# Hymba-style layer: window heads mixed side by side in one tile per token half, and four pieces of work in another order

## The chip, the cores and the metric

The kernel runs on one core of one Trainium2 chip. A core has a matrix engine (TensorE, here PE, with its weight loads as PEld), a vector engine (VectorE, DVE), a scalar engine (ScalarE, ACT), a general engine (GpSimd, POOL) and a synchronisation engine (SyncE, SP) that mostly issues transfers. Each runs its own list of instructions in order and waits on semaphores for the others. The metric is the device time of one execution in microseconds (us); lower is better.

## The reference

One layer over 1024 tokens of width 1024, in fp32. A normed input feeds one projection whose columns go to two token mixers: a sliding-window attention with 8 query heads in two groups of four, each group with one key/value head, and a 2-D neighbourhood attention with 8 heads. Then come an output projection, a gated MLP with a convolution of width 3 and a last norm.

```python
hn = rmsnorm(h, norm_mix[l])
proj = jnp.einsum('bsd,de->bse', hn, w_in[l])
qa, ka, va, qb, kb, vb = jnp.split(proj, splits, axis=-1)
qa = partial_rope(qa.reshape(B, S, A_HEADS, HEAD_DIM), cos, sin)
ka = partial_rope(ka.reshape(B, S, A_KV_HEADS, HEAD_DIM), cos, sin)
o_a = window_gqa_sink(qa, ka, va, sink[l])          # |i-j| <= 128, blocks of 128 tokens
o_b = neighbourhood_attention(qb, kb, vb, rpb[l])   # 16 x 64 grid, bias rpb per head
mix = jnp.concatenate([rmsnorm(o_a, norm_a[l]), rmsnorm(o_b, norm_b[l])], axis=-1)
h = h + jnp.einsum('bse,ed->bsd', mix, w_out[l])
hn = rmsnorm(h, norm_ffn[l])
h = h + conv_gated_mlp(hn, w_gate[l], w_up[l], conv_w[l], conv_b[l], w_down[l])
```

## The kernel before, in words

Everything is held transposed: channels on the 128 partitions, the 1024 tokens in the columns, two token halves of 512 columns. A projection job takes 128 output channels; its fp32 weight is split into a high part (`whi`, ACT, L156) and a low part (`wlo`, L157, DVE or POOL), and three matrix products (L172, L173, L174) add high by high, high by low and low by high. A job's weight comes in two halves of four input tiles: `load` and later `load_rest`. Jobs 0, 1 and 2 run before the window attention; the later jobs fill PE between attention steps.

The first three tiles are turned (the partial rotation) by a fold: L285 copies the rotating rows into a small tile `f` by DMA, DVE does four operations (L287 to L289), and L291 copies the rows back (`t<-f`). For the third tile the small tile is called `turns`. The SP queue issues most of these transfers, in its order. Then the tiles are split into high and low stacks: `split_first_k` (L316 to L319), `split_first` (L309, L310) and `split_pair` (L297 to L302).

A unit of window attention is a group g and a block b of 128 tokens. PE makes scores (L434), DVE takes a masked minimum with a bias (L464, result `nm`), ACT takes the exponential (L468) with its sum, DVE inverts it (L469, `sm`). The probabilities then go one of several ways to a 16-bit transposed pair: over POOL (L472, then L478, L479), over DVE (L482, L483, L485), over POOL with a scratch tile `y` (L488, L489), each to a transposing DMA (L490, `turned`), or, path T, over PE (L496) with ACT and DVE taking the result out of PSUM (L499, L500). PE multiplies by the values (L523), and `leave` adds the two 64-partition halves of the bank `o`: ACT copies two heads across (L534) and DVE adds two heads one at a time (L538) into tiles `mix[2g]` and `mix[2g+1]`, each 128 x 1024, named `mixa` in the profile.

The neighbourhood attention of a head h works the same way (L598 is its product with the values) with a bias tile `xb`, built by POOL from a gathered table in two subtractions (L556, L557). `bias_tiles(0)` is built early, and step 4 of head h asks for the tile of head h+1; `bias_tiles(1)` is also there early. Then follow the squares of the mixed heads (L211 through `squares`), the norm's gains (L871), a split into 16-bit halves (L200, L201) and the output projection.

PE's order is written out by hand, step by step. The orders of DVE, ACT, POOL and SP come from a scheduler that follows the program's order and priorities: `tc.high_priority` moves an instruction ahead, and `behind("name")` keeps what is in it behind a marked instruction in the engines' lists.

Of the kernel before, what the change touches and what calls it, by code (L numbers as in the profile page):

```python
# [17 lines left out]
AF = mybir.ActivationFunctionType  # L18
ALU = mybir.AluOpType
# [44 lines left out]
def hybrid_layer(tc, xT, w_in, w_out, w_gate, w_up, w_down, small, sink, rpb, consts, rope, out):  # L64
    nc = tc.nc
    with ExitStack() as ctx:
# [86 lines left out]
        def halve_w(raw):  # L153

            hi, lo = (wpool.tile([128, 4, 128], F32R, name=n, tag=n) for n in ("whi", "wlo"))
            mark["weights"] = nc.scalar.activation(hi, raw, AF.Copy)  # L156
            mark["weights low"] = (nc.gpsimd if mark.get("attention") or mark.get("early") else nc.vector).tensor_tensor(lo, raw, f32(hi[:, :, :]), op=ALU.subtract)  # L157
            return [(hi[:, j, :], lo[:, j, :]) for j in range(4)]

        def load_w(src):  # L160
# [116 lines left out]
        def rotate(t, n, order=()):  # L277

            m = slice(0, n)
            f, u = folded[0]  # L280
            folded.append(folded.pop(0))
            rows = lambda s: t[4 * s:n:8].rearrange("a (c w) -> a c w", w=128)
            fold = lambda s: f[m, s]
            for s in range(2):
                (nc.scalar, nc.sync)[s].dma_start(fold(s), rows(s))  # L285
            for s in range(2):
                nc.vector.tensor_tensor(u[m, s], f[m, 1 - s], rs[m, s], op=ALU.mult)  # L287
            nc.vector.tensor_tensor(f[m], f[m], rc[m], op=ALU.mult)
            mark["turned"] = nc.vector.tensor_tensor(f[m], f[m], u[m], op=ALU.add)  # L289
            with behind(*order):  # L290
                back = [nc.sync.dma_start(rows(s), fold(s)) for s in range(2)]  # L291
            mark["back"] = back[1]

        def split_pair(t, early=False):

# [88 lines left out]
            return [v[:, i].rearrange("p c s w -> p c (s w)") for i in range(n // 64)], up  # L384

        qa, ka, va, qb, kb, vb = {}, {}, {}, {}, {}, {}
        mix = [None] * 8

        def turn(m, t):
            g, i = divmod(m, 3)  # L390
# [59 lines left out]
        class Rows:  # L450
# [5 lines left out]
            def softmax(self, path, j, ps, n, bias, nsink=None, skip=0):  # L456

                c = n // 128
                with tc.high_priority(offset=50):
# [9 lines left out]
                    nc.vector.reciprocal(sm, sm)  # L469
                    x = apart(p[:, 0:n])  # L470
                    if path in "PT":
                        nc.gpsimd.tensor_scalar(x, x, sm, P_TOP, op0=ALU.mult, op1=ALU.mult)  # L472
                    if path == "T":
                        return lambda: self.turn(j, p, c, skip)
                    hl = staged()
# [26 lines left out]
        def unit_window(g, b):  # L502
# [26 lines left out]
            def leave():  # L529
                ot = apool.tile([128, 2, 128], F32, name="ot", tag="ot", bufs=1, padded_shape=[128, 4, 128])  # L530
                o4 = st["o"][:, :].rearrange("p (j w) -> p j w", w=128)
                for e in range(2):
                    me, other = slice(64 * e, 64 * e + 64), slice(64 - 64 * e, 128 - 64 * e)
                    nc.scalar.activation(ot[me], o4[other, e::2, :], AF.Copy)  # L534
                    for i in range(2):
                        if mix[2 * g + i] is None:
                            mix[2 * g + i] = big("mixa", "mix")
                        nc.vector.tensor_tensor(mix[2 * g + i][me, b * 128:(b + 1) * 128], o4[me, e + 2 * i, :], ot[me, i, :], op=ALU.add)  # L538

            return [q_step(j) for j in range(4)], [v_step(i, k) for k in range(2) for i in range(len(cs))], [lambda j=j: turn[j]() for j in range(4) if PATH_A[j] == "T"]  # L540

        def bias_tiles(h):

            raw = apool.tile([128, RAW_LEN], F32, name="rr", tag="rr", bufs=1)
            src = bass.AP(tensor=rpb.tensor, offset=rpb.offset + h * RPB_LEN, ap=[[RPB_W, ROWS], [1, 8], [1, RAW_LEN]])
            nc.sync.dma_start(raw, src)
            x = apool.tile([128, 5, 128], F32, name="xb", tag="xb")
            a = raw[:, 0:1]
            view = lambda d0, step, n: bass.AP(
                tensor=a.tensor, offset=a.offset + RAW_LEN - 1 - 8 * (d0 + 1),  # L550
                ap=[list(a.ap[0]), [-8 * step, n], [-RPB_W, ROWS], [-1, 8]])
            mk = cst[:, K_MB:K_MB + 384].rearrange("p (v r c) -> p v r c", r=ROWS, c=8)
            far = mk[:, 1:2]
            far = bass.AP(tensor=far.tensor, offset=far.offset, ap=[list(far.ap[0]), [0, 2], [8, ROWS], [1, 8]])
            xv = x[:, :, :].rearrange("p v (r c) -> p v r c", c=8)
            nc.gpsimd.tensor_tensor(xv[:, 1:4], mk, view(-1, 1, 3), op=ALU.subtract)  # L556
            nc.gpsimd.tensor_tensor(xv[:, 0::4], far, view(-1, 2, 2), op=ALU.subtract)  # L557
            return x

        bias_of = {}  # L560
# [63 lines left out]
        class Project:  # L624
# [10 lines left out]
            def run(self):  # L635
# [7 lines left out]
                else:  # L643

                    ps = [bank("pj", "pj") for _ in range(2)]
                    for h, k in [(h, i - 3 * h) for i in range(KT + 3) for h in range(2) if 0 <= i - 3 * h < KT]:
                        block(ps[h], self.w[k], xg[k], h, k == 0, k == KT - 1)
                        yield
                        if h and k % 2:
                            mg[k // 2] = split16(mix[k // 2], "xg")  # L650
                        if k == KT - 1:
                            with tc.high_priority(offset=500):
                                evacuate(self.t, ps[h], h, self.grid)
# [139 lines left out]
        for h in range(2):  # L793
            evacuate(third.t, ps3[h], h, False)
        with tc.high_priority(offset=400):
            with behind("turned"):
                turn(third.m, third.t)
            with behind("value"):
                nc.scalar.activation(warm, eps, AF.Exp)
# [25 lines left out]
        def rest():  # L825
            for i, job in enumerate(jobs[1:]):
# [15 lines left out]
                        aux[i, n]()  # L842
                if i == 0:
                    with behind("stack", "copied"):
                        mark["early"] = True
                        jobs[2].load_rest()
                        mark["early"] = False
                    with behind("weights"):
                        make_stacks(third)
                if isinstance(job, Project):  # L850
# [4 lines left out]
                        yield False  # L855

        def square_a():
            norm["sq"] = squares(mix[0:4], 2, ups[0:4])

        def narrow_a(h):  # L860
            norm["v", h] = inverse_power(norm["sq"][:, tsl(h)], 512, "pt")
# [5 lines left out]
            nc.scalar.activation(norm["a"][:, tsl(h)], widen(norm["v", h], "pt"), AF.Copy)  # L867

        def normed_a(i, h):
            x = lambda: mix[i][:, tsl(h)]  # L870
            return lambda: nc.vector.scalar_tensor_tensor(  # L871
                x(), x(), gains[:, i:i + 1], norm["a"][:, tsl(h)], op0=ALU.mult, op1=ALU.mult)

# [1023 lines left out]
```

## Time and profile before

| | |
|---|---|
| median of 3 runs | 1031.53 us (1031.27 to 1031.98) |
| profiled execution | 1031.43 us, its span 1029.6 us |
| granted clock of PE | 0.998 |
| PE busy | 1009.7 us (98%) |
| DVE busy | 878.2 us (85%) |
| ACT busy | 676.7 us (66%) |
| POOL busy | 216.6 us (21%) |

The stages by time, in the span: to about 58 us the first projections and folds; to about 200 us the window attention; from 181 to 343 us the neighbourhood attention beside it and after it, with projections between the steps; to about 413 us the output projection and its norm; then the gate, up and down products to the end. Times in the rows are from the span's start. A row's idle time is what stood empty before the instruction on its engine, with the engine, tile and line that ended it.

### The profile page before, as it was taken

Reading aid. Unit: us, or ns where it says so; the run is one execution under the profiler, and the core shown is the slowest. Engines: PE = TensorE matmul, PEld = TensorE weight load, DVE = VectorE, ACT = ScalarE, POOL = GpSimd, SP = SyncE. Lnnn points to the kernel's source line nnn. Section 1 sums busy time; section 2 is a strip of 40 time slices with the busy share of each in tenths; the row PEclk is TensorE's granted clock in tenths of the full one; section 3 lists DMA queues with packets and bytes.
Section 4 is the critical chain, followed back from the end, with each engine's and each line's share of the span. In section 5 each row is a group of like instructions: output and inputs, shape, how many; then the busy total and the mean of one; then the engine's idle time right before and its main releaser. Section 6 shows DMA issues by size and latency. Waiting matters only on the chain.

```text
span 1029.6 us, 15701 instructions
## 1 busy us (share of the span) xinstructions
PE 1009.7 (98%) x5102; PEld 576.6 (56%) x5102; DVE 878.2 (85%) x1746; ACT 676.7 (66%) x1242; POOL 216.6 (21%) x340
## 2 busy tenths in 40 slices
PE   8999999999999999999999999999999999999996
PEld 6877777777875545544444444444444444444446
DVE  7799998766898799899897988898888879999874
ACT  8567787768687587645777777754634657655551
POOL 2244555767876310001000000000000000000002
PEclk9999999999999999999999999999999999999999
DMA  8557474787699765201787867733232779978834
GB/s 319 191 136 138 100 152 99 146 167 133 138 192 219 261 251 194 83 1 42 235 276 250 273 233 256 235 113 133 82 113 102 256 243 307 308 244 268 258 140 164
DMA packets 143939, 191.80 MB, mean 186 GB/s; under 512 B 77360, under 2 KB 88112, under 8 KB 143856
## 3 DMA queue, kind: packets, MB, share of 16 engines
q1 hardware_dynamic: 133264, 164.84, 56.1%
q10 hardware_dynamic: 10592, 25.95, 6.5%
q8 instruction: 40, 0.66, 0.2%
q14 instruction: 43, 0.35, 0.1%
HBM read 132.81 MB, written 28.57 MB: 157 GB/s over the span
## 4 chain that ended last, share of the span: by engine, by line
PE 73%; DVE 5%; DMA 1%; ACT 1%; issue 1%; POOL 0%; ACTq 0%; DVEq 0%; POOLq 0%
PE dn L1185 6%; PE dn L1186 6%; PE dn L1187 6%; PE pj L180 6%; PE z L1185 5%; PE z L1186 5%; PE z L1187 5%; PE y L1185 4%; PE y L1186 4%; PE y L1187 4%; PE x L1185 4%; PE x L1186 4%; PE x L1187 4%; PE pj L172 2%; PE pj L174 2%; PE pj L173 2%
## 5 line engine op out<-in xcount | busy, mean ns | idle before, releaser
L1187 PEld LDWEIGHTS <-wlo 128*128 128x128 f16 x898 | 87.8, 98 | 101.4 <-issue 0.2
L1185 PEld LDWEIGHTS <-whi 128*128 128x128 f16 x898 | 88.1, 98 | 100.3
L1186 PEld LDWEIGHTS <-whi 128*128 128x128 f16 x898 | 87.8, 98 | 100.2
L1187 PE MATMUL dn<-xd,wlo 128*128 128x512 f16 (+1 forms) x330 | 120.4, 365 | 0.0
L1186 PE MATMUL dn<-xd,whi 128*128 128x512 f16 (+1 forms) x330 | 120.4, 365 | 0.0
L1185 PE MATMUL dn<-xd,whi 128*128 128x512 f16 (+1 forms) x330 | 120.4, 365 | 0.0
L172 PE MATMUL pj<-xgh,whi 128*128 128x512 f32 x248 | 106.7, 430 | 0.0
L1185 PE MATMUL z<-hg,whi 128*128 128x512 f16 x264 | 100.1, 379 | 0.0
L1186 PE MATMUL z<-hg,whi 128*128 128x512 f16 x264 | 100.1, 379 | 0.0
L1187 PE MATMUL z<-hg,wlo 128*128 128x512 f16 x264 | 100.1, 379 | 0.0
L468 ACT ACTIVATE p<-p,nm 128x385 f32<-128x385 f32 (+3 forms) x128 | 74.8, 585 | 36.8 <-DVE nm L464 33.9
L174 PE MATMUL pj<-xgh,wlo 128*128 128x512 f32 x248 | 97.9, 395 | 0.0
L173 PE MATMUL pj<-xgl,whi 128*128 128x512 f32 x248 | 97.4, 393 | 0.0
L1159 ACT ACTIVATE whi<-ws,m 128x512 f16<-128x512 f32 (+1 forms) x96 | 65.9, 708 | 37.9 <-DVE ws L1326 21.9
L1160 DVE SCALAR_TENSOR_TENSOR wlo<-ws,m,whi 128x512 f16<-128x512 f32 (+1 forms) x96 | 70.1, 739 | 20.4 <-ACT whi L1159 20.2
L1040 POOL TENSOR_TENSOR back<-back,cst 128x4 f32<-128x4 f32 (+1 forms) x7 | 2.8, 394 | 356.9 <-DVE back L1039 356.9
L1174 ACT ACTIVATE scan<-scan 128x1024 f32<-128x1024 f32 (+1 forms) x60 | 61.0, 1017 | 19.4 <-DMA scan<-in_w_down_dram 13.0
L1159 ACT ACTIVATE whi<-raw,m 128x512 f16<-128x512 f32 (+1 forms) x78 | 51.3, 699 | 18.1 <-DMA raw<-in_w_down_dram 11.2
L1160 DVE SCALAR_TENSOR_TENSOR wlo<-raw,m,whi 128x512 f16<-128x512 f32 (+1 forms) x78 | 55.3, 731 | 6.9 <-ACT whi L1159 6.8
L1187 PE MATMUL y<-hg,wlo 128*128 128x512 f16 x160 | 60.6, 379 | 0.0
L1185 PE MATMUL y<-hg,whi 128*128 128x512 f16 x160 | 60.6, 379 | 0.0
L1186 PE MATMUL y<-hg,whi 128*128 128x512 f16 x160 | 60.6, 379 | 0.0
(298 smaller groups left out, 2460.8 us busy)
## 6 DMA issues: line engine op xcount, KB each, us to landing
xd<-x SPq DMA_DIRECT2D x77, 256.0 KB, 5.2
raw<-in_w_down_dram SPq DMA_DIRECT2D x64, 256.0 KB, 3.2
x<-c ACTq DMA_DIRECT2D x22, 512.0 KB, 4.0
scan<-in_w_gate_dram SPq DMA_DIRECT2D x18, 512.0 KB, 5.3
scan<-in_w_up_dram SPq DMA_DIRECT2D x18, 512.0 KB, 5.6
raw<-in_w_gate_dram SPq DMA_DIRECT2D x18, 512.0 KB, 4.4
raw<-in_w_up_dram SPq DMA_DIRECT2D x18, 512.0 KB, 3.4
raw<-in_w_in_dram SPq DMA_DIRECT2D x32, 256.0 KB, 3.3
```

Of the source, the lines that this page charges most:

```text
L172: nc.tensor.matmul(ps, w[0], x[0][:, tsl(h)], start=first, stop=False)
L173: nc.tensor.matmul(ps, w[0], x[1][:, tsl(h)], start=False, stop=False)
L174: nc.tensor.matmul(ps, w[1], x[0][:, tsl(h)], start=False, stop=last)
L180: nc.tensor.matmul(ps, a, b, start=i == 0 and b is x[h][0] and a is w[0], stop=i == len(ws) - 1 and a is w[1])
L468: nc.scalar.activation(p[:, 0:e], p[:, 0:e], AF.Exp, bias=nm, scale=-1.0, accum_out=sm)
L1040: nc.gpsimd.tensor_tensor(back, back, unit_back.to_broadcast([128, n]), op=ALU.mult)
L1159: mark["whi"] = nc.scalar.activation(hi, src, AF.Copy, scale=by)
L1160: nc.vector.scalar_tensor_tensor(lo, src, by, hi, op0=ALU.mult, op1=ALU.subtract)
L1174: nc.scalar.activation(t, t, AF.Square, accum_out=dst)
L1185: nc.tensor.matmul(ps, w[0], x[0], start=first and i == 0, stop=False, skip_group_check=True)
L1186: nc.tensor.matmul(ps, w[0], x[1], start=False, stop=False, skip_group_check=True)
L1187: nc.tensor.matmul(ps, w[1], x[0], start=False, stop=last and i == len(ws) - 1, skip_group_check=True)
```

## The change

Four edits. In `leave` one tile `mixa[g, half]` per group and token half holds two heads' pairs side by side (2 x 512 columns), and one DVE addition writes both; the squares, the gains and the split read these tiles. The turn of the third tile is issued behind the first tile's last write-back as well ("first back"). The second half of job 4's weight, `jobs[2].load_rest()`, makes its low part on DVE at high priority, no longer on POOL. And the bias tiles of heads 1 to 7 are built behind the last scaling of probabilities on POOL (L472) that the program has issued by then.

```diff
@@ -154,7 +154,7 @@
 
             hi, lo = (wpool.tile([128, 4, 128], F32R, name=n, tag=n) for n in ("whi", "wlo"))
             mark["weights"] = nc.scalar.activation(hi, raw, AF.Copy)
-            mark["weights low"] = (nc.gpsimd if mark.get("attention") or mark.get("early") else nc.vector).tensor_tensor(lo, raw, f32(hi[:, :, :]), op=ALU.subtract)
+            mark["weights low"] = (nc.gpsimd if mark.get("attention") else nc.vector).tensor_tensor(lo, raw, f32(hi[:, :, :]), op=ALU.subtract)
             return [(hi[:, j, :], lo[:, j, :]) for j in range(4)]
 
         def load_w(src):
@@ -290,6 +290,7 @@
             with behind(*order):
                 back = [nc.sync.dma_start(rows(s), fold(s)) for s in range(2)]
             mark["back"] = back[1]
+            mark.setdefault("first back", back[1])
 
         def split_pair(t, early=False):
 
@@ -384,7 +385,8 @@
             return [v[:, i].rearrange("p c s w -> p c (s w)") for i in range(n // 64)], up
 
         qa, ka, va, qb, kb, vb = {}, {}, {}, {}, {}, {}
-        mix = [None] * 8
+        mix, mixa = [None] * 8, {}
+        mixed = lambda k, h: mixa[k // 2, h][:, tsl(k % 2)]
 
         def turn(m, t):
             g, i = divmod(m, 3)
@@ -469,7 +471,7 @@
                     nc.vector.reciprocal(sm, sm)
                     x = apart(p[:, 0:n])
                     if path in "PT":
-                        nc.gpsimd.tensor_scalar(x, x, sm, P_TOP, op0=ALU.mult, op1=ALU.mult)
+                        mark["scaled"] = nc.gpsimd.tensor_scalar(x, x, sm, P_TOP, op0=ALU.mult, op1=ALU.mult)
                     if path == "T":
                         return lambda: self.turn(j, p, c, skip)
                     hl = staged()
@@ -532,10 +534,10 @@
                 for e in range(2):
                     me, other = slice(64 * e, 64 * e + 64), slice(64 - 64 * e, 128 - 64 * e)
                     nc.scalar.activation(ot[me], o4[other, e::2, :], AF.Copy)
-                    for i in range(2):
-                        if mix[2 * g + i] is None:
-                            mix[2 * g + i] = big("mixa", "mix")
-                        nc.vector.tensor_tensor(mix[2 * g + i][me, b * 128:(b + 1) * 128], o4[me, e + 2 * i, :], ot[me, i, :], op=ALU.add)
+                    if (g, b // 4) not in mixa:
+                        mixa[g, b // 4] = big("mixa", "mix")
+                    dst = mixa[g, b // 4][:, :].rearrange("p (i w) -> p i w", i=2)[me, :, b % 4 * 128:(b % 4 + 1) * 128]
+                    nc.vector.tensor_tensor(dst, o4[me, e::2, :], ot[me, 0:2], op=ALU.add)
 
             return [q_step(j) for j in range(4)], [v_step(i, k) for k in range(2) for i in range(len(cs))], [lambda j=j: turn[j]() for j in range(4) if PATH_A[j] == "T"]
 
@@ -553,8 +555,9 @@
             far = mk[:, 1:2]
             far = bass.AP(tensor=far.tensor, offset=far.offset, ap=[list(far.ap[0]), [0, 2], [8, ROWS], [1, 8]])
             xv = x[:, :, :].rearrange("p v (r c) -> p v r c", c=8)
-            nc.gpsimd.tensor_tensor(xv[:, 1:4], mk, view(-1, 1, 3), op=ALU.subtract)
-            nc.gpsimd.tensor_tensor(xv[:, 0::4], far, view(-1, 2, 2), op=ALU.subtract)
+            with behind(*["scaled"] * (h > 0)):
+                nc.gpsimd.tensor_tensor(xv[:, 1:4], mk, view(-1, 1, 3), op=ALU.subtract)
+                nc.gpsimd.tensor_tensor(xv[:, 0::4], far, view(-1, 2, 2), op=ALU.subtract)
             return x
 
         bias_of = {}
@@ -647,7 +650,9 @@
                         block(ps[h], self.w[k], xg[k], h, k == 0, k == KT - 1)
                         yield
                         if h and k % 2:
-                            mg[k // 2] = split16(mix[k // 2], "xg")
+                            part = split16(mixa[k // 4, k // 2 % 2], "xg")
+                            for i in range(2):
+                                mg[2 * (k // 4) + i] = (mg[2 * (k // 4) + i] or ()) + (part[i],)
                         if k == KT - 1:
                             with tc.high_priority(offset=500):
                                 evacuate(self.t, ps[h], h, self.grid)
@@ -793,7 +798,7 @@
         for h in range(2):
             evacuate(third.t, ps3[h], h, False)
         with tc.high_priority(offset=400):
-            with behind("turned"):
+            with behind("turned", "first back"):
                 turn(third.m, third.t)
             with behind("value"):
                 nc.scalar.activation(warm, eps, AF.Exp)
@@ -842,9 +847,8 @@
                         aux[i, n]()
                 if i == 0:
                     with behind("stack", "copied"):
-                        mark["early"] = True
-                        jobs[2].load_rest()
-                        mark["early"] = False
+                        with tc.high_priority(offset=500):
+                            jobs[2].load_rest()
                     with behind("weights"):
                         make_stacks(third)
                 if isinstance(job, Project):
@@ -855,7 +859,15 @@
                         yield False
 
         def square_a():
-            norm["sq"] = squares(mix[0:4], 2, ups[0:4])
+            acc = None
+            for k in range(4):
+                s2 = tmp("sq")
+                for h in range(2):
+                    nc.scalar.activation(s2[:, tsl(h)], mixed(k, h), AF.Square, scale=ups[k])
+                    if acc is not None:
+                        nc.vector.tensor_tensor(s2[:, tsl(h)], s2[:, tsl(h)], acc[:, tsl(h)], op=ALU.add)
+                acc = s2
+            norm["sq"] = acc
 
         def narrow_a(h):
             norm["v", h] = inverse_power(norm["sq"][:, tsl(h)], 512, "pt")
@@ -867,7 +879,7 @@
             nc.scalar.activation(norm["a"][:, tsl(h)], widen(norm["v", h], "pt"), AF.Copy)
 
         def normed_a(i, h):
-            x = lambda: mix[i][:, tsl(h)]
+            x = lambda: mixed(i, h)
             return lambda: nc.vector.scalar_tensor_tensor(
                 x(), x(), gains[:, i:i + 1], norm["a"][:, tsl(h)], op0=ALU.mult, op1=ALU.mult)
 
```

The first fold on SP (`f` and `turns` are the small fold tiles, `t` the turned tiles; 8x8x128 is half of the first tile, 16x8x128 half of the second). Before:

```order
L291 DMA t<-f 8x8x128
L285 DMA turns<-t 128x1x128
L291 DMA t<-f 8x8x128
L291 DMA t<-f 16x8x128 x2
L291 DMA t<-turns 16x8x128 x2
```

and now:

```order
L291 DMA t<-f 8x8x128 x2
L285 DMA turns<-t 128x1x128
L291 DMA t<-f 16x8x128 x2
L291 DMA t<-turns 16x8x128 x2
L379 DMA_TRANSPOSE v<-vhl 128x16x64
```

The first tile's second half is written back ahead of the third tile's read. On DVE, where the first stacks are made and the first scores are taken, before:

```order
L318 TENSOR_TENSOR ka<-t,ka 64x1024
L310 SCALAR_TENSOR_TENSOR q<-t,q 64x1024 x2
L269 TENSOR_TENSOR t<-pj,rstd_370 128x512
L299 SCALAR_TENSOR_TENSOR t<-t,q 128x1024
L464 ISA p,nm<-s,cst,nsink 128x256
L464 ISA nm 128x1
L269 TENSOR_TENSOR t<-pj,rstd_370 128x512
L464 ISA p,nm<-s,cst,nsink 128x256
```

and now, where L311, L300 and L466 are what L310, L299 and L464 were:

```order
L319 TENSOR_TENSOR ka<-t,ka 64x1024
L311 SCALAR_TENSOR_TENSOR q<-t,q 64x1024 x2
L269 TENSOR_TENSOR t<-pj,rstd_370 128x512
L157 TENSOR_TENSOR wlo<-raw,whi 128x512
L300 SCALAR_TENSOR_TENSOR t<-t,q 128x1024
L157 TENSOR_TENSOR wlo<-raw,whi 128x512
L466 ISA p,nm<-s,cst,nsink 128x256
L466 ISA nm 128x1
L466 ISA p,nm<-s,cst,nsink 128x256
L466 ISA nm 128x1
L287 TENSOR_TENSOR f<-f,turns 64x128 x2
```

The first L157 is the low part that POOL made; the second one stood further behind, as did the L287 of the next fold. On POOL, in the first grid head, before:

```order
L472 TENSOR_SCALAR p<-p,sm 128x384
L157 TENSOR_TENSOR wlo<-raw,whi 128x512
L488 TENSOR_SCALAR y<-p,sm 128x384
L489 TENSOR_TENSOR stage<-y,stage 128x3x128
L488 TENSOR_SCALAR y<-p,sm 128x384
L157 TENSOR_TENSOR wlo<-raw,whi 128x512
L489 TENSOR_TENSOR stage<-y,stage 128x3x128
```

and now, L474, L490 and L491 being L472, L488 and L489:

```order
L474 TENSOR_SCALAR p<-p,sm 128x384
L559 TENSOR_TENSOR xb<-cst,rr 128x384
L157 TENSOR_TENSOR wlo<-raw,whi 128x512
L560 TENSOR_TENSOR xb<-cst,rr 128x2x128
L490 TENSOR_SCALAR y<-p,sm 128x384
L491 TENSOR_TENSOR stage<-y,stage 128x3x128
L490 TENSOR_SCALAR y<-p,sm 128x384
L157 TENSOR_TENSOR wlo<-raw,whi 128x512
```

The two bias pieces of head 1 stood in the first projections and now stand here. Further on, at the bias of head 7, POOL before:

```order
L489 TENSOR_TENSOR hl<-y,hl 128x3x128
L556 TENSOR_TENSOR xb<-cst,rr 128x384
L557 TENSOR_TENSOR xb<-cst,rr 128x2x128
L472 TENSOR_SCALAR p<-p,sm 128x384
L488 TENSOR_SCALAR y<-p,sm 128x256
```

and now:

```order
L491 TENSOR_TENSOR hl<-y,hl 128x3x128
L474 TENSOR_SCALAR p<-p,sm 128x384
L559 TENSOR_TENSOR xb<-cst,rr 128x384
L560 TENSOR_TENSOR xb<-cst,rr 128x2x128
L490 TENSOR_SCALAR y<-p,sm 128x384
```

The scaling that a PE transposition waits for has changed places with the two bias pieces. PE's list has the same instructions in the same order as before.

## The prediction

> **What bounds the kernel now.** I read the page's busy time first, then the busy time by stretches, then the waits of PE, then the rows around each wait. The profiled execution took 1031.43 us, of which 1029.6 us are its span and 1.83 us lie around it; the median of the three runs, 1031.53 us, is 0.10 us above it. A measurement of this kernel can tell about 0.2% from no change, here 2.06 us, and "faster" and "slower" mean more than that.
>
> ```profile
> PE 1009.7 (98%) x5102; PEld 576.6 (56%) x5102; DVE 878.2 (85%) x1746; ACT 676.7 (66%) x1242; POOL 216.6 (21%) x340
> ```
>
> TensorE (PE) is busy for 98%, and the change leaves its instructions and their order as they are. So it can only act on the 2% in which PE waits, and only in the stages it touches: the first three projections and both attentions. By stretches (us; busy time of PE, PEld, DVE, ACT, POOL; clock; DMA share; GB/s):
>
> ```profile
> 60.00:80.00 20.00, 17.43 (x87) 13.87 (x87) 18.49 (x58) 12.85 (x31) 9.63 (x19) 1.00 0.63 142
> 100.00:150.00 50.00, 48.97 (x283) 36.69 (x282) 46.12 (x159) 40.06 (x105) 27.17 (x56) 1.00 0.62 123
> 150.00:200.00 50.00, 48.92 (x282) 37.26 (x282) 41.45 (x145) 37.41 (x95) 29.10 (x51) 1.00 0.59 117
> 200.00:260.00 60.00, 60.00 (x329) 47.16 (x328) 41.27 (x129) 43.74 (x97) 43.59 (x55) 1.00 0.74 149
> 300.00:340.00 40.00, 37.46 (x223) 23.07 (x223) 33.06 (x100) 31.28 (x72) 26.88 (x35) 1.00 0.95 206
> ```
>
> PE idles 2.57 us in 60 to 80, 1.03 in 100 to 150, 1.08 in 150 to 200, nothing in 200 to 260 and 2.54 in 300 to 340. The clock is 1.00 throughout, so it is no part of this. DVE, at 46.12 of 50 us, is the engine with the least room while the windowed attention runs. What PE waits for from 40 to 340 us (us in total, times, longest):
>
> ```profile
> PE pt L496 <- POOL p L472: 1.9, 3, 1.0
> PE o L523 <- DVE by L482: 1.2, 1, 1.2
> PE o L598 <- DMA turned<-stage: 1.0, 1, 1.0
> PE o L523 <- DVE mixa L538: 0.6, 1, 0.6
> PE pt L496 <- DVE turned L500: 0.6, 1, 0.6
> PE wm L255 <- DVE nm L464: 0.5, 1, 0.5
> PE o L598 <- DMA turned<-hl: 0.5, 1, 0.5
> PE s L434 <- DMA q<-t: 0.3, 1, 0.3
> PE s L434 <- DVE nm L464: 0.3, 1, 0.3
> ```
>
> These 6.9 us are nearly the whole field. The change can win some of them or add to them.
>
> **The first fold and the weight's low part (46 to 80 us).** Here an SP queue row, the ACT row behind it, and the DVE, POOL and PE rows of the disputed time (start, duration; in brackets the idle time before and its releaser), then durations by line (min/median/max in ns):
>
> ```profile
> 44.83 0.65 SPq L291 DMA_DIRECT2D t<-f  x1
> 46.84 0.57 SPq L285 DMA_DIRECT2D turns<-t  x1
> 47.45 1.95 SPq L291 DMA_DIRECT2D t<-f  x3
> 49.57 1.06 ACT L316 ACTIVATE ka<-t 64x1024 fp32r<-64x1024 f32 x1 [1.90 <-DMA t<-f]
> 50.25 0.49 DVE L287 TENSOR_TENSOR turns<-turns 128x128 f32<-128x128 f32 x2 [1.67 <-DMA turns<-t]
> 54.55 3.45 DVE L310 SCALAR_TENSOR_TENSOR q<-t,q 64x1024 fp32r<-64x1024 f32 x2
> 54.61 2.30 POOL L157 TENSOR_TENSOR wlo<-raw,whi 128x512 fp32r<-128x512 f32 x1 [8.25 <-ACT whi L156]
> 56.97 0.19 PEld L174 LDWEIGHTS pj<-xgh,wlo 128*128 128x128 f32 x1 [0.31 <-POOL wlo L157]
> 58.02 0.69 DVE L269 TENSOR_TENSOR t<-pj,rstd 128x512 f32<-128x512 f32 x1
> L310 DVE SCALAR_TENSOR_TENSOR q<-t,q x2: 1211/1708/2204, 54.5 to 55.8; 64x1024 fp32r<-64x1024 f32 x2
> L157 DVE TENSOR_TENSOR wlo<-raw,whi x16: 670/686/1194, 14.1 to 151.9; 128x512 fp32r<-128x512 f32 x16
> L157 POOL TENSOR_TENSOR wlo<-raw,whi x16: 1284/1292/2299, 54.6 to 283.7; 128x512 fp32r<-128x512 f32 x16
> ```
>
> SP's second t<-f, half of the first tile's fold, stood behind turns<-t from 44.83+0.65 = 45.48 to 47.45, though its data were ready with the first half's. Now it goes first, and ACT's L316, which waited 1.90 us for it, may start up to 1.9 us sooner. But L316 is not what DVE waits for: DVE's idle time ends at 50.25 with turns<-t, which was released at 46.84 and still is; from 50.25 to 58.02 DVE has no gap. So the earlier ACT is worth nothing by itself; the cover is DVE's own queue, and the most it could be worth without it is 1.9 us.
>
> The low part is another matter. POOL's one took 2.30 us where 1.29 is usual, the second L310 beside it 2.20 where the first took 1.21: the two held one another up, one waiting while the other ran. The Trainium skill, "SBUF — State Buffer", section "SBUF: two separate sides", says why: a VectorE operation with two SBUF inputs and a GpSimd operation that reads SBUF share an exclusive lock on a port pair, held for a whole instruction. By that rule, too, these two should be kept apart; the trace agrees with 2.30 and 2.20 us.
>
> With POOL idle there, the L310s take 2 x 1.21 = 2.42 in place of 3.45, a gain of 1.03. DVE then does the L269 (0.69) and the low part (0.69), so it stands 1.03-0.69 = 0.34 us ahead afterwards. PE, however, waits for this low part in order, and everything behind L174 with it: 54.55+2.42+0.69+0.69 = 58.35, against 56.97 now. That is 1.4 us of new wait. It takes the place of the next two waits (0.3 for a score bank, 0.3 for q<-t), so PE arrives about 0.8 us late at 75 us, where it now waits 0.6 for L500 and then 1.2 for a DVE instruction. There 1.8 us of waits can swallow 0.8, and what remains is set by DVE, 0.34 us ahead less a 64-partition fold or two that moved forward in its queue. I take a gain of 0.3 us. Ends: a loss of 0.8 if DVE is held by the later PE and not the reverse, a gain of 1.5 if the earlier ACT also shortens DVE's waits for vhl.
>
> **The mix as one tile (80 to 200 us).** 64 adds of 64x128 become 32 of 64x2x128; squares, gains and splits later read the same number of elements in as many instructions.
>
> ```profile
> L538 DVE TENSOR_TENSOR mixa<-o,ot x64: 260/285/295, 81.9 to 196.9; 64x128 f32<-64x128 f32 x64
> 104.42 0.50 DVE L538 TENSOR_TENSOR mixa<-o,ot 64x128 f32<-64x128 f32 x2
> 102.61 0.28 DVE L538 TENSOR_TENSOR mixa<-o,ot 64x128 f32<-64x128 f32 x1
> 75.47 0.42 DVE L500 TENSOR_TENSOR turned<-pt,turned 128x256 f16<-128x256 f32 x1
> ```
>
> No row shows the merged add. Its nearest row, a 256-column add that reads PSUM, takes 0.42. A pair in a row takes 0.50, a pair apart 2 x 0.285 = 0.57, so 0.08 to 0.15 us goes per pair, 32 times: 2.6 to 4.8 us of DVE. This can reach PE only through its waits. The four adds that release an accumulator bank become two that end sooner together; the 0.6 us at L538 is that wait, and I count it gone. Of the three L472 waits (1.9) one is the 1.0 treated below; the other 0.9 are late softmaxes behind a full DVE, and I count 0.7. The wm wait of 0.5 ends a DVE chain: 0.4. Together 1.7 us; the ends are 0.3 (other instructions move into the freed time) and 2.1, all that PE idles in 100 to 200.
>
> **The bias of head 1 (187 us).** In 42 to 45 us POOL loses 2 instructions that nothing waited for. They return between L472 and the y/stage pairs of the first grid head.
>
> ```profile
> L556 POOL TENSOR_TENSOR xb<-cst,rr x8: 992/1004/1516, 36.9 to 305.7; 128x384 f32<-128x384 f32 x8
> L557 POOL TENSOR_TENSOR xb<-cst,rr x8: 713/732/1193, 37.8 to 306.7; 128x256 f32<-128x256 f32 x8
> 187.00:196.00 9.00, 8.46 (x47) 6.49 (x45) 7.37 (x22) 8.17 (x20) 8.41 (x10) 1.00 0.80 148
> L328 DVE SCALAR_TENSOR_TENSOR kb<-t,cst,ka x16: 722/880/1560, 135.9 to 308.6; 128x512 fp32r<-128x512 f32 x16
> ```
>
> POOL is busy 8.41 of these 9 us, so 1.00+0.73 = 1.73 us is late for whatever comes next: a weight's low part, y, stage, and the transposes issued on SP after each stage. The cover is that PE has other work in its queue and no wait at all in 200 to 260. I charge 0.1, with ends of 0 and 2.6 (in the rivals).
>
> **The bias of head 7 (306 us).**
>
> ```profile
> 305.73 1.00 POOL L556 TENSOR_TENSOR xb<-cst,rr 128x384 f32<-128x384 f32 x1
> 306.66 1.19 POOL L557 TENSOR_TENSOR xb<-cst,rr 128x256 f32<-128x256 f32 x1
> 307.83 0.58 POOL L472 TENSOR_SCALAR p<-p,sm 128x384 f32<-128x384 f32 x1
> 315.64 3.56 DMA turned<-hl
> 326.64 6.28 DMA turned<-stage
> ```
>
> L472 now runs before the two bias pieces, at about 305.7, and PE's wait of 1.0 us goes. But the next y and stage start when they did, since the sum of POOL's work is the same, and the last two rows, from the chain of waits, show transposes at 315.64 and 326.64 that PE waits for (0.5 and 1.0) and that no PE instruction releases. PE comes earlier and waits longer there. I count 0.2, ends 0 and 1.0.
>
> **Sum.** 0.3 + 1.7 - 0.1 + 0.2 = 2.1 us: 1031.43 - 2.1 = 1029.3 for a profiled execution, 1029.4 us as a median.
>
> **Rivals.**
>
> Given back: DVE's gain is filled by other work and the moved waits turn up again at the next transposes, leaving 0.3 to 1 us: 1030.8. For it: 200 to 260 shows that PE fills a stage by itself, and the chain of waits at 315 and 326 is DMA. Against it: the L538 wait has DVE alone behind it.
>
> Slower: POOL at 187 us. If the transposes behind the stages have less than 1.73 us to spare, the delay passes to PE in full, and if L328 meets one more POOL instruction it takes 1.56 in place of 0.72, another 0.84: 2.6 in all, against at most 1.0 gained before. This gives 1031.5-0.6+2.6 = 1033.5. It decides from the point where a transpose lands after PE reaches its L598. For it: POOL's 8.41 of 9 us. Against: 60.00 of 60 us with no wait right after. The port rule of the Trainium skill named above (its page's section "Who interferes with whom") speaks for this rival, since it makes a GpSimd operation in a busy VectorE stretch block whole instructions; the 1560 ns beside 722 of L328 agree.
>
> Larger: the fold brings 1.0, the mix 1.8 and head 7's wait comes off in full, 1.0, because the transposes also move ahead: 3.8 less, 1027.7. For it: DVE leads into the transposes of 315. Against: between them lie only SP and POOL.
>
> That the change does nothing, because PE's waits only move, is part of the first rival.
>
> **How the numbers follow.** Forecast 0.55, of which 0.36 lies below the 0.2% line at 1029.47 and 0.19 above; its own range is 1028.0 to 1030.4. Given back 0.20, all within 0.2%. Larger 0.14, all faster. Slower 0.11, of which 0.09 is over 0.2%. So faster 0.50, same 0.41, slower 0.09. The range for 8 in 10 runs from 1027.3, in the middle of the larger case, to 1031.9, which leaves out most of the slower one.
>
> **What would show it.** Right: DVE's second L310 at about 1.2 us; a new PE wait of about 1.4 us for a DVE low part near 57 us and less than 1.8 us of waits in 75 to 80; merged adds of 0.40 to 0.44 us; no wait for mixa; no POOL wait near 307, and longer ones at L598 near 319 and 333. Wrong: PE still 0.8 us or more behind at 80 us; new waits at L598 between 196 and 205; merged adds near 0.55 us; idle time of PE from 100 to 200 still about 2 us.

## The result, and the profile after

The changed kernel takes 1028.44 us in the median of 13 runs (1027.76 to 1030.12), the kernel before 1031.76 us (13 runs, 1031.09 to 1033.01). The ratio is 0.9967 with a 95% interval of 0.9960 to 0.9974: 3.4 us faster by the ratio (3.3 by the medians), by more than the 0.2% that can be told apart. A few executions on record took far longer (1157.37 to 4899.26 us, all but the longest at a lower granted clock); the ratios leave them out, and so do the medians given for `no_bias_rest` and `no_fold`. The profiled execution has a span of 1026.6 us, 3.0 us less. The forecast was 1029.4 us with 2.1 us of gain: the direction held and the time lies in the range, but the terms of the sum were not those that the traces show.

The stretches of the profile after (us; busy time of PE, PEld, DVE, ACT, POOL; clock; DMA share; GB/s):

```profile
60.00:80.00 20.00, 18.44 (x95) 15.08 (x94) 18.25 (x56) 13.14 (x32) 7.66 (x21) 1.00 0.64 140
100.00:150.00 50.00, 49.04 (x285) 37.17 (x284) 46.13 (x146) 40.80 (x107) 26.34 (x57) 1.00 0.62 126
150.00:200.00 50.00, 49.35 (x282) 37.75 (x281) 39.86 (x138) 37.01 (x95) 30.61 (x52) 1.00 0.56 117
200.00:260.00 60.00, 60.00 (x329) 47.01 (x328) 41.23 (x123) 43.10 (x95) 45.62 (x55) 1.00 0.76 152
300.00:340.00 40.00, 38.80 (x233) 23.63 (x232) 32.17 (x98) 30.55 (x71) 26.08 (x36) 1.00 0.98 206
```

PE's idle time falls from 2.57 to 1.56 us in 60 to 80 and from 2.54 to 1.20 in 300 to 340. From 100 to 200 it falls only from 2.11 to 1.61. The waits of PE from 40 to 420 us after the change:

```profile
PE o L525 <- DVE by L484: 1.4, 1, 1.4
PE pt L498 <- POOL p L474: 1.4, 3, 0.7
PE pj L180 <- DVE mg L1144: 1.2, 1, 1.2
PE o L601 <- DMA turned<-hl: 0.6, 1, 0.6
PE o L601 <- DMA turned<-stage: 0.5, 1, 0.5
PE pt L498 <- DVE turned L502: 0.3, 1, 0.3
PE wm L255 <- DVE nm L466: 0.2, 1, 0.2
```

There is no wait for the weight's low part, none for mixa and none for q<-t. The waits for POOL's scaling are three again, but none of 1.0 and none near 305 us.

Because PE runs the same list, one can ask for any matrix instruction how much earlier it starts than before. The next table is worked out from the starts of the PE rows of both traces. Each column is the change of that difference within a stage (us; minus is gained). The first 45 us hold almost nothing of the four edits, and what they show there (-0.24 to +0.52, over all kernels) is taken as the spread of single executions; after 420 us it is mostly of the same size. The four columns between are what to compare. From 340 to 420 us the difference changes by 0.01 or less, but for +0.29 in `no_bias_rest` and +0.32 in `no_fold`. The names are those of the experiments below.

```
kernel           0-45  45-80  80-200  200-300  300-340
after           +0.51  -1.89   -0.27    -0.03    -1.41
bias1_only      +0.28  -0.38   -0.14    +0.00    -0.23
bias_rest_only  -0.03  +0.34   +0.03    +0.01    -0.95
fold_only       +0.02  -0.09   +0.04    +0.01    -0.13
mix_only        +0.17  -0.07   +0.19    -0.02    +0.04
wlo_only        -0.24  -0.25   +0.90    +0.00    +0.82
bias1_wlo       +0.46  -1.86   +0.67    +0.00    +0.84
bias_wlo        +0.15  -1.87   +0.64    +0.04    -1.02
no_bias1        +0.18  -0.51   +0.43    -0.03    -0.48
no_bias_rest    +0.52  -1.86   -0.21    -0.03    -0.25
no_wlo          +0.28  -0.37   +0.29    -0.02    -1.76
no_mix          +0.43  -1.87   +0.61    +0.00    -1.12
no_fold         +0.12  -1.88   -0.26    -0.03    -1.11
```

So the change gains 1.9 us before 80 us, 0.3 in the window attention and 1.4 from 300 to 340 us.

### The profile page after: what moved, and what is told of

Its sections match the earlier page's. It is cut to its first block, busy times and chain, and to the rows that moved or that the text cites. A ratio compares the mean times of both kernels' runs of the same rounds, so it can differ in the third digit from the quotient of the medians.

```text
span 1026.6 us, 15663 instructions
## 1 busy us (share of the span) xinstructions
PE 1009.0 (98%) x5102; PEld 577.2 (56%) x5102; DVE 875.2 (85%) x1715; ACT 675.8 (66%) x1242; POOL 214.6 (21%) x339
## 4 chain that ended last, share of the span: by engine, by line
PE 75%; DVE 3%; DMA 2%; ACT 1%; issue 0%; POOL 0%; DVEq 0%; ACTq 0%; POOLq 0%
PE pj L180 7%; PE dn L1199 6%; PE dn L1198 6%; PE dn L1197 6%; PE z L1197 5%; PE z L1198 5%; PE z L1199 5%; PE x L1197 4%; PE y L1197 4%; PE x L1198 4%; PE y L1198 4%; PE y L1199 4%; PE x L1199 4%; PE pj L172 3%; PE pj L174 2%; PE pj L173 2%
```

## The experiments

Twelve kernels were run, each in five rounds against the kernel before. Single edits came first.

**Head 1's bias alone, and the other heads' alone.** The edit of the bias tiles moves two different things, so it was taken apart:

```diff
+            with behind(*["scaled"] * (h == 1)):      # bias1_only
+            with behind(*["scaled"] * (h > 1)):       # bias_rest_only
                 nc.gpsimd.tensor_tensor(xv[:, 1:4], mk, view(-1, 1, 3), op=ALU.subtract)
                 nc.gpsimd.tensor_tensor(xv[:, 0::4], far, view(-1, 2, 2), op=ALU.subtract)
```

> The kernel before with only the bias tile of head 1 built behind the window attention's scalings. By the prediction's steps its leaving the start is worth nothing and its coming back at 187 us costs 0.1: 0 to +0.1 us, PE at 80 us where it was before. By the reading of the trace after, the two bias pieces at 42 to 44 us held DVE up (low part 1.19 us in place of 0.69, fold step 0.95 in place of 0.41), and DVE's list decides until 80 us: about 1 us faster, PE about 1 us ahead at 80 us. By the rival that POOL at 187 us decides: slower by up to 2.6 us, with new waits of PE between 195 and 206 us.

Measured: 1030.86 us against 1031.41, ratio 0.9994 (0.9985 to 1.0002). Neither forecast is met in the time: PE gains only 0.38 us by 80 us. But DVE shows what the move does. Rows in order of time (start, duration) of the kernel before, with POOL's bias piece beside DVE, and then of DVE with head 1's bias moved:

```profile
42.12 1.26 POOL L556 TENSOR_TENSOR xb<-cst,rr 128x384 f32<-128x384 f32 x1 [3.55 <-DMA rr<-in_rpb_dram]
42.73 1.19 DVE L157 TENSOR_TENSOR wlo<-raw,whi 128x512 fp32r<-128x512 f32 x1
43.85 0.95 DVE L289 TENSOR_TENSOR f<-f 64x256 f32<-64x256 f32 x1
46.12 0.69 DVE L269 TENSOR_TENSOR t<-s,rstd 128x512 f32<-128x512 f32 x1
```

```profile
43.08 0.69 DVE L157 TENSOR_TENSOR wlo<-raw,whi 128x512 fp32r<-128x512 f32 x1
43.69 0.41 DVE L289 TENSOR_TENSOR f<-f 64x256 f32<-64x256 f32 x1
45.42 0.69 DVE L269 TENSOR_TENSOR t<-s,rstd 128x512 f32<-128x512 f32 x1
48.41 0.49 DVE L287 TENSOR_TENSOR turns<-turns 128x128 f32<-128x128 f32 x2 [0.52 <-DMA turns<-t]
...
60.17 0.69 DVE L269 TENSOR_TENSOR t<-pj,rstd 128x512 f32<-128x512 f32 x1 [1.14 <-PE pj L174]
```

Low part and fold step fall from 1.19 and 0.95 to 0.69 and 0.41. The third tile's fold starts at 48.41 in place of 50.25. Of these 1.84 us, 0.71 are DVE's own: the tile is sent to the fold at 46.13 in place of 46.84. The other 1.13 are a quicker transfer, which the last section takes up. DVE is up to 1.8 us early, and then loses it: further on its list has L269, which needs a projection that PE finishes when it always did, at about 60 us. There is no new wait of PE between 195 and 206 us, so POOL's fuller stretch at 187 us costs nothing.

> The kernel before with only the bias tiles of heads 2 to 7 built later, behind a scaling. By the prediction's steps the scaling near 306 us comes ahead and PE gives the gain back at the next transposes: -0.2 us (0 to -1.0). By the reading of the trace after, the whole bias leaves 305 us, POOL's products and the transposes behind them move up too, and nothing is given back: -1.4 us, PE's lead growing from 300 to 340 us. No difference before 200 us by either.

Measured: 1030.79 us against 1031.41, ratio 0.9997 (0.9988 to 1.0006); PE gains 0.95 us from 300 to 340. The time cannot tell it, the trace of the one profiled execution can. POOL in this kernel, near the place that the prediction costs at 0.2:

```profile
304.66 1.01 POOL L489 TENSOR_TENSOR hl<-y,hl 128x384 f16<-128x384 f32 x1 [0.51 <-POOL y L488]
305.66 0.58 POOL L472 TENSOR_SCALAR p<-p,sm 128x384 f32<-128x384 f32 x1
306.22 0.47 POOL L488 TENSOR_SCALAR y<-p,sm 128x256 f32<-128x256 f32 x1
307.32 0.68 POOL L489 TENSOR_TENSOR stage<-y,stage 128x256 f16<-128x256 f32 x1 [0.63 <-ACT stage L483]
```

The bias pieces do not follow the scaling here. They come behind the next one, at 315.55, and y and stage move up by 2.2 us (L488 at 306.22, before at 308.39), and with them the transposes that PE waits for. All waits of PE in this stage:

```profile
306.61 0.38 PE L599 MATMUL o<-turned,v 128*128 128x256 f16 x2 [1.32 <-DMA turned<-stage]
332.36 0.38 PE L599 MATMUL o<-turned,v 128*128 128x256 f16 x2 [0.20 <-DMA turned<-stage]
```

Before, PE waited 1.00 us for the scaling (at 308.47), then 0.52 (319.34) and 1.02 (332.97) for transposes. One new wait of 1.32 us gives part back, and the rest stays won. In the whole change the last bias tile is likewise not at 305 but here:

```profile
312.08 0.58 POOL L474 TENSOR_SCALAR p<-p,sm 128x384 f32<-128x384 f32 x1
312.63 0.98 POOL L559 TENSOR_TENSOR xb<-cst,rr 128x384 f32<-128x384 f32 x1
313.56 0.72 POOL L560 TENSOR_TENSOR xb<-cst,rr 128x256 f32<-128x256 f32 x1
```

So the piece of POOL's list that is shown under the change as head 7's is one scaling further on than the piece before; the sentence there that scaling and bias only changed places is wrong.

**The fold's order alone.**

```diff
+            mark.setdefault("first back", back[1])
...
-            with behind("turned"):
+            with behind("turned", "first back"):
                 turn(third.m, third.t)
```

> The kernel before with only the first tile's write-back ahead of the third tile's read. By the prediction's steps 0 us, since DVE waits for the third tile's transfer at 50.25 us and not for ACT. The rival: the transfer of the third tile, 3.4 us from issue to landing before and 2.0 us after the whole change, is quicker because this order is another: DVE's idle time of 1.67 us ends 1 us or more sooner, and the kernel is 0.5 to 1.4 us faster.

Measured: 1031.27 us against 1031.41, ratio 0.9997 (0.9988 to 1.0006). ACT's first stack starts at 47.74 us in place of 49.57, and DVE's idle time before the third tile ends at 50.17, before at 50.25:

```profile
50.17 0.29 DVE L287 TENSOR_TENSOR turns<-turns 128x128 f32<-128x128 f32 x1 [1.40 <-DMA turns<-t]
47.74 1.06 ACT L317 ACTIVATE ka<-t 64x1024 fp32r<-64x1024 f32 x1
```

An earlier ACT is worth nothing there, as the prediction had it; the rival, with its 1 us or more, falls.

**The mix tiles alone.** The `leave`, squares, split and gains of the change, and nothing else.

```diff
...
-                    for i in range(2):
...
-                        nc.vector.tensor_tensor(mix[2 * g + i][me, b * 128:(b + 1) * 128], o4[me, e + 2 * i, :], ot[me, i, :], op=ALU.add)
...
+                    nc.vector.tensor_tensor(dst, o4[me, e::2, :], ot[me, 0:2], op=ALU.add)
...
```

> The kernel before with only the mix as one tile per token half. By the prediction's steps 1.7 us faster (0.3 to 2.1), the merged add at about 0.42 us and no wait of PE for mixa near 105 us. By the reading of the trace after, where PE's lead grew by 0.3 us from 80 to 200 us and new waits for POOL's scalings stood at 133, 141 and 173 us: 0.3 us faster at most, with the old waits replaced by others.

Measured: 1031.71 us against 1031.41, ratio 1.0002 (0.9993 to 1.0011). The group of the merged add in this kernel (instructions; least, median and largest ns; from when to when):

```profile
L539 DVE TENSOR_TENSOR mixa<-o,ot x32: 395/422/428, 82.0 to 196.1; 64x256 f32<-64x256 f32 x32
```

The stretch from 80 to 200 us, with the columns of the first table, in the kernel before and in this one, and then the wait of this one's PE for POOL's scaling:

```profile
80.00:200.00 120.00, 117.89 (x677) 89.14 (x676) 106.44 (x365) 93.82 (x242) 66.95 (x130) 1.00 0.63 125
80.00:200.00 120.00, 117.83 (x675) 89.19 (x674) 105.03 (x335) 93.99 (x242) 65.59 (x130) 1.00 0.61 125
```

```profile
PE pt L497 <- POOL p L473: 2.5, 4, 1.0
```

The merged add takes 0.422 us, as estimated, and DVE is busy 105.03 us of the 120 us, before 106.44. The wait for mixa is gone and nothing is gained: PE is busy 117.83 us, before 117.89, and the waits for POOL's scaling grow from 1.9 us to 2.5.

**The weight's low part alone, and the change without it.**

```diff
-                        mark["early"] = True
-                        jobs[2].load_rest()
-                        mark["early"] = False
+                        with tc.high_priority(offset=500):
+                            jobs[2].load_rest()
```

> The kernel before with only the weight's low part on DVE, at high priority. By the prediction's steps PE waits about 1.4 us for it near 57 us, most of which later waits swallow: a gain of 0.3 us, between a loss of 0.8 and a gain of 1.5. Theory S, that this edit alone carries the gain of the first 80 us in the trace after: PE 1.9 us ahead at 80 us. Theory I, that it needs the bias of head 1 out of the way: DVE's list starts 1 to 2 us later than in the whole change, PE waits 1 us or more near 57 us, and PE is at most 1 us ahead at 80 us.

Measured: 1033.28 us against 1031.55, ratio 1.0019 (1.0010 to 1.0027): slower by 2.0 us by the ratio (1.7 by the medians). The instructions of this kernel in order of time, and below them a row of its PE's waits:

```profile
54.34 2.46 DVE L310 SCALAR_TENSOR_TENSOR q<-t,q 64x1024 fp32r<-64x1024 f32 x2
57.45 0.68 DVE L157 TENSOR_TENSOR wlo<-raw,whi 128x512 fp32r<-128x512 f32 x1
58.18 0.50 PE L174 MATMUL pj<-xgh,wlo 128*128 128x512 f32 x1 [1.34 <-DVE wlo L157]
```

```profile
PE o L598 <- DMA turned<-stage: 1.7, 1, 1.7
```

The two stacks take 2.46 us for 3.45, and the new wait is 1.34 us where the prediction reckoned 1.4. By 80 us the later waits have swallowed it and 0.25 us is left as a gain, where 0.3 was reckoned. What is lost comes later: 0.90 us from 80 to 200 and 0.82 near 330 us, where the wait for a transpose is 1.7 us in place of 1.0. The profiled execution loses another 1.45 us between 420 and 600 us, where nothing was edited; that is not explained, and in the other kernels this stretch changes by 0.12 at most. Theory S, that this edit carries the early gain, falls.

> The whole change, but with the weight's low part on POOL as before. Theory S: the gain to 80 us is gone, PE at 80 us where it was before, 1.9 us slower than the whole change. Theory I, that DVE's lead from the bias of head 1 is lost where DVE waits for PE near 60 us (1.14 us when that bias alone was moved) unless the low part's edit puts other work there: the same here, 1.3 to 1.9 us slower than the whole change. By the prediction's steps 0.3 us slower.

Measured: 1029.96 us against 1031.55, ratio 0.9983 (0.9974 to 0.9992). The gain to 80 us is down to 0.37 and DVE waits 1.13 us for PE at 60 us as with head 1's bias alone.

**The whole change without head 1's bias, and without the other heads'.** The condition of the first diff is `h > 1` and `h == 1`.

> The whole change, but with the bias tile of head 1 built early as before. Theory S: as fast as the whole change. Theory I: POOL's pieces at 42 to 44 us hold DVE up again by 1 us, its stacks end 1 to 2 us later, PE waits near 57 us for the low part, and 0.8 to 1.5 us of the gain to 80 us is lost. By the prediction's steps 0.1 us faster than the whole change.

Measured: 1031.36 us against 1031.55, ratio 0.9997 (0.9988 to 1.0005): without this one edit the change gains nothing that can be measured. The low part on DVE in this kernel, in order of time, then its row of PE's waits, and last DVE in the whole change:

```profile
42.84 1.27 DVE L157 TENSOR_TENSOR wlo<-raw,whi 128x512 fp32r<-128x512 f32 x1
57.58 0.68 DVE L157 TENSOR_TENSOR wlo<-raw,whi 128x512 fp32r<-128x512 f32 x1
```

```profile
PE pj L174 <- DVE wlo L157: 1.0, 1, 1.0
```

```profile
48.01 0.29 DVE L287 TENSOR_TENSOR turns<-turns 128x128 f32<-128x128 f32 x1 [0.25 <-DMA turns<-t]
53.11 2.46 DVE L311 SCALAR_TENSOR_TENSOR q<-t,q 64x1024 fp32r<-64x1024 f32 x2
56.21 0.68 DVE L157 TENSOR_TENSOR wlo<-raw,whi 128x512 fp32r<-128x512 f32 x1
```

56.21+0.68 = 56.89 us is in time for PE, 57.58+0.68 = 58.26 is not.

> The whole change, but with the bias tiles of heads 2 to 7 built as early as before. If the later stage's gain is theirs, PE's lead stops growing at 300 us: 0.9 to 1.4 us slower than the whole change, with a wait of PE for POOL's scaling of 1 us near 305 us. By the prediction's steps 0.2 us slower.

Measured: 1029.32 us against 1031.55, ratio 0.9978 (0.9969 to 0.9988). The gain from 300 to 340 us falls from 1.41 to 0.25 us, and PE's wait for POOL's scaling there is back:

```profile
PE pt L498 <- POOL p L474: 1.1, 1, 1.1
```

**The pairs.** The kernel before with the low part's edit and head 1's bias (`h == 1`), or with all bias tiles (`h > 0`), and neither mix tiles nor the fold's order.

> The kernel before with the bias of head 1 late and the weight's low part on DVE, nothing else; DVE, ACT and PE have the same lists as with the low part alone. Theory I, that the two edits need one another: PE 1.3 to 2 us ahead at 80 us and no wait for the low part near 57 us, where each edit alone left it 0.1 and 0.5 us ahead; 1.3 to 2 us faster than before, though the low part alone was 1.9 us slower. If the two are independent: the sum of the two, about 1.3 us slower than before.

Measured: 1030.88 us against 1031.43, ratio 0.9995 (0.9986 to 1.0004). PE is 1.86 us ahead at 80 us, as Theory I has it and as neither edit alone is (0.38 and 0.25). The time does not show it, because 0.67 us goes from 80 to 200 and 0.84 from 300 to 340 us, at a wait of 1.8 us for one transpose:

```profile
PE o L599 <- DMA turned<-stage: 1.8, 1, 1.8
```

So the theory was right on the first 80 us and wrong that they pass to the end by themselves.

> The kernel before with all bias tiles late and the low part on DVE: the whole change without the mix tiles and without the fold's order. If these two edits carry the whole: 3 us faster than before, as the whole change. By the prediction's steps, where the mix carries 1.7 of 2.1 us: 0.4 us faster.

Measured: 1029.26 us against 1031.43, ratio 0.9980 (0.9971 to 0.9989), neither forecast: 2.1 us, between the two. With the other heads' tiles late the stage from 300 to 340 us turns from a loss of 0.84 to a gain of 1.02.

**The whole change without the mix tiles, and without the fold's order.**

> The whole change with the mix in four tiles as before, 64 adds. By the prediction's steps 1.7 us slower than the whole change (0.3 to 2.1), with the wait for mixa near 105 us back. By the mix alone, which changed nothing that can be measured (1.0002): as fast as the whole change within 0.5 us.

Measured: 1029.85 us against 1031.43, ratio 0.9982 (0.9973 to 0.9991), about 1.5 us less gain by the ratios, whose intervals just touch. By the trace the mix tiles are worth 0.88 us from 80 to 200 (-0.27 with them, +0.61 without) and a little from 300 to 340. Alone they were worth nothing. That they pay where PE has come early and meets DVE fits this, but no run shows it apart.

> The whole change with the first tile's second half written back behind the third tile's read, as before. By the prediction's steps equal to the whole change, as long as DVE and not ACT decides. The rival: with DVE's list 2 us earlier than before, ACT's stacks come too late for it in the old order, DVE waits for ACT's first stack and 0.3 to 0.8 us of the gain to 80 us is lost.

Measured: 1028.39 us against 1031.43, five executions, ratio 0.9969 (0.9957 to 0.9982): as fast as the whole change. The gain to 80 us is 1.88. The rival of a late ACT falls too: without the edit the stack starts at 48.47 us, and DVE needs it only at 49.96.

```profile
48.47 1.06 ACT L316 ACTIVATE ka<-t 64x1024 fp32r<-64x1024 f32 x1 [1.91 <-DMA t<-f]
49.96 1.21 DVE L317 TENSOR_TENSOR kb<-t,ka 64x1024 fp32r<-64x1024 f32 x1
```

No kernel was measurably faster than the whole change.

## Why the prediction was right or wrong

**The total.** 2.1 us were forecast and 3.4 measured. The sign and the range hold, but this is not a confirmation of the sum: two terms were too small and one too large. Set against the columns of the table, they were off by 1.6, 1.2 and 1.4 us, the last the other way. That the total still fell into the range is in part luck. The time, 1028.44 us, lies a little nearer to the 1027.7 of the rival "larger" than to the forecast's 1029.4.

Of the signs, the stacks, the merged adds and the missing waits for mixa and near 307 us came as said. The wait of 1.4 us for the low part did not, and the waits at L598 did not grow: the one near 319 is gone, the one near 333 is 0.55 in place of 1.02 us, and a new one of 0.65 stands at 309.01.

**The first 80 us: 0.3 forecast, 1.9 by the trace.** The step that failed is "POOL loses 2 instructions that nothing waited for". Nothing waited for their results, but DVE ran beside them: its low part and fold step took 2.14 us in place of 1.10, and the third tile was evacuated and sent to its fold 0.7 to 0.8 us later than without the two. So the step "released at 46.84 and still is" falls too: in the change it is 46.01. The transfer itself was then quicker by 1.1 us with head 1's bias alone and by 1.4 in the whole change, for the reasons in the last section, so more than half of DVE's lead at the third tile comes from there. The prediction reads exactly this kind of mutual delay at 54 us and does not look for it at 42, though the row of L157, with its largest value of 1194 ns, was quoted. The rule of the Trainium skill, "SBUF — State Buffer", section "SBUF: two separate sides", that one of the two blocks for a whole instruction, bears here as at 54 us; this trace agrees with 1.19 against 0.69 us for the same low part.

The other steps of that part held. The stacks fell to 2.46 us (2.42), the new wait was 1.34 us (1.4) in the kernel with that edit alone, and 0.25 us (0.3) was left at 80 us. In the whole change that wait never arises, since DVE starts early enough. And the early DVE alone is worth 0.38 us, since its next instruction waits for PE. That the two edits pay fully only together, 1.86 us against 0.38 and 0.25, was in no case of the prediction.

**The mix tiles: 1.7 forecast, 0.3 in its stage.** The size of the merged add was right (0.422 us). The step that failed is that PE's waits were taken as debts of DVE: "the other 0.9 are late softmaxes behind a full DVE, and I count 0.7". With the tiles alone the adds are busy 13.4 us in place of 16.6, but DVE as a whole only 1.41 us less, since other work moved into the stretch, as the term's low end had it. PE's waits moved instead of ending: before, 0.39 and 0.54 us for POOL's scaling at 114.56 and 158.53; with the tiles, 0.32, 0.69 and 0.41 at 134.98, 143.07 and 174.80. In the whole change, too, three such waits of 1.4 us in all remain. What the tiles bring, 0.88 us, they bring only beside the other edits; which of these they need is not shown. "Given back", the first rival, describes the mix alone.

**Head 1's bias at 187 us: 0.1 of cost forecast, none found.** No wait at L598 between 195 and 206 us in any run with it; the nearest is 0.17 us at 191.38 in `no_bias_rest`. The slower rival did not come about by this mechanism. A slower kernel was among the experiments all the same, by the low part alone.

**The later bias tiles: 0.2 forecast, about 1.2.** The step that failed is "the next y and stage start when they did, since the sum of POOL's work is the same". It rests on a misread list: the tile of head 7 passes two scalings and the three products y between them, not one scaling (those of heads 2 to 6 pass one or two, and also three y), and its two pieces, 1.00 and 1.19 us, leave the place before the transposes. PE's gain there is 1.41 us with them late and 0.25 without. The rival "larger" had this ("the transposes also move ahead") as one of its parts, and the prediction argued against it.

**The fold's order: nothing, as forecast,** both alone and within the change, by the time. In the single trace without it the gain from 300 to 420 us is 0.6 us smaller, which the time does not bear out.

## What to carry to other kernels

An instruction whose result nobody awaits can still cost: look at what runs beside it on the other engine and at which transfer it delays, and compare each duration with the usual one of the same line before an edit is costed at nothing. Where engines run fixed lists, an edit that makes one engine early pays only when the next entry of its list is ready too; two edits that are worth 0.4 and 0.2 us alone were worth 1.9 together by 80 us of the trace, and one of them alone made the kernel slower. For moved work, find both places by counting the same instruction on both lists, not by a similar neighbourhood.

## What the runs showed of the hardware

The two halves of the third tile are sent to the fold by SP and ACT at the same instant, 64 KB each. In the six kernels with head 1's bias early, DVE's first instruction on them came 3.1 to 4.0 us after that (46.84 to 50.25 before, 47.03 to 50.17 with the fold's order alone, 46.60 to 50.57 with the other heads' bias alone). In the eight where that bias was late it took 2.0 to 2.3 us (46.01 to 48.01 after, 46.13 to 48.41 with that bias alone). No instruction of the bias stands in that time. The fold's order is worth 0.3 us of it at most: with the new order the first packet of ACT's half goes 1.2 us after the issue, with the old one 1.5.

The traces show what differs. ACT's half goes as 144 packets of the queue q10. Near it stands one packet of 16 KB that the profile calls `instruction`, on q8, which takes 0.9 to 1.5 us. The next rows count the packets that start in a stretch (queue, kind: packets, MB, share of 16 engines). The first two are of the kernel before, from 46.84 to 48.34 us, where q10 has none yet, and from 48.82 to 49.50. The last two are of the kernel with head 1's bias alone, from 46.14 to 48.085, where q8 has none yet, and from 48.085 to 48.20.

```profile
q8 instruction: 1, 0.02, 3.9%
q10 hardware_dynamic: 8, 0.00, 4.0%
q10 hardware_dynamic: 144, 0.07, 13.7%
q8 instruction: 1, 0.02, 51.5%
```

Before, the instruction packet runs from 47.73 to 48.67 us. Most of the transfer is through by 48.80, but its last eight packets follow one by one until 49.48, and the landing is at 50.23. With head 1's bias late all 144 are through at 48.08, the instruction packet starts at 48.09, and the landing is at 48.38. So it is in every kernel: in the six slower transfers the instruction packet starts 0.3 to 0.7 us ahead of the first packet of q10, in the eight quicker ones behind the last. With the fold's order alone nine packets straggle, a sixteenth of 144. That they share one of the 16 DMA engines with the instruction packet is inferred from this number, since the trace does not name a packet's engine. Up to 0.5 us of the difference lies between the last packet and the landing, and that part is not explained. Sending the tile 0.7 to 0.8 us earlier thus went with a transfer quicker by 1.1 us, and in the whole change by 0.3 more from the fold's order. No kernel sets this order on purpose, without any bias work.
